# Two seams of a transformer layer: the last values' copy behind the first weight casts, and the feed-forward's first operands half a token tile sooner

## The chip, the cores and the metric

The kernel runs on one core of a Trainium2 chip. The metric is the device time of one execution in microseconds (us). Three executions of the kernel before took 3070.08, 3070.73 and 3071.90; their median, 3070.73 us, is the time before. One further execution was taken with the profiler; it took 3072.42 us, and its trace spans 3070.6 us.

The core's engines work side by side, each through its own instructions in order: TensorE (PE) multiplies matrices into the PSUM banks, VectorE (DVE) and ScalarE (ACT) do elementwise work, GpSimd (POOL) helps, and the SP queue issues most transfers (DMA). ACT issues a few transfers of its own.

## The reference

One layer over 2048 latent tokens of width 1024, with 256 context tokens. Cut to what matters:

```
x = x + g1 * branch_merge(attn_x, gm_x, ga_x, gb_x, w_br_attn, w_br_gm, w_out)

def branch_merge(attn_o, gm_o, ga_logit, gb_logit, w_br_attn, w_br_gm, w_out):
    y = sigmoid(ga_logit) * (attn_o @ w_br_attn) + sigmoid(gb_logit) * (gm_o @ w_br_gm)
    return y @ w_out

h2 = modulate(x, norm2_g, sh2, sc2)          # RMSNorm, scale, shift
x = x + g2 * (square(relu(h2 @ w_ff1)) @ w_ff2)
```

`attn_x` is softmax attention of 8 query heads over 2304 keys; `gm_x` is a gated branch. All data are float32.

## The kernel before

**Precision and products.** Every product of float32 matrices is made of three passes: each operand is split into a high part (a cast, on ACT) and a low part (the difference, on DVE or POOL), and PE adds high x high, high x low and low x high (`mm3`, L181, in the merge; `product`, L1541, in the feed-forward). The feed-forward's matrices are moreover multiplied by a scheme of seven block products: out of the four quarters of each operand come seven sums, numbered 0 to 6, and seven products are taken in the order 0, 1, 5, 6, 4, 2, 3 or near it. Each of these sums is split again into a high and a low half (`halves`, L1359). An operand of the left side has four pieces, one per 128 of the 512 channels (HK = 4).

**Stages.** Projections; attention (`attend`, L1109), in units of one block of 512 tokens and two heads; the merge (`merge`, L1240); then the feed-forward (`ffn`, L1767) in two blocks of 1024 tokens, each as a first half `ff1` and a second half `ff2`.

**The end of the attention.** `values` (L2114) adds the weighted values of a unit in one PSUM bank, `self.o`. `leave` (L2141) copies it to SBUF on ACT and stores it to `at_d` on ACT's queue. For the last unit, this stands at the end of `attend`, directly behind the last values. The merge then begins with loads (`load`), the split of the branch weights of its first step (`cast(0, "dve")`: two casts on ACT, two differences on DVE), and the first weight load for the output product.

**The merge.** For each of four blocks of 512 tokens there are eight steps (branch products, gates, y), and then the output product: four token tiles `tt` of 128 tokens, each in two halves `n` of 512 columns, 24 passes per half. The results are multiplied by a gain and added to the residual row on DVE (L1345, L1346; below called the residual add); when both halves of a row tile are in, `stored` (L1265) writes it to `x1_d` through SP's queue (L1266) and squares it on ACT (L1269). `stored` for tile `tt` is called at `(tt + 1, 0)`, behind that half's products. Between the halves a side generator takes a step, ahead of the residual add of that half (L1341 to L1346).

**The side generator of the last block** is `h_first` (L1403): it prepares the operands of the first feed-forward block from `x1_d`. Piece by piece (`kk`) it loads x (`x1_load`, four transfers, L1377), scales it (`x1_scaled`, one DVE instruction of 128x2048, L1385), transposes it on PE into four banks and copies these to SBUF on ACT with scale and shift (`x1_turned`, L1391, the copy is L1398), and forms the sums (`sums`, L1409). The steps are: load 0; then for each piece "scale, and the sums of the piece before" and "turn, and load the next". `w1_ops` (L1477) prepares the weights of a feed-forward group, also in steps: load (L1482), high and low part of the first half (L1493, L1494), two sums (L1499 to L1504), their splits (L1508, L1509), the last split (L1514, L1515). In `merge` before, the fourth piece is turned, and the weights' first cast made, only behind the merge's last product.

**Order.** Instructions go to each engine's list by a planner that takes them by the order in which the program wrote them, as operands and tile slots come free in its own time model. `order` (L1863) restricts it: instructions of a pinned range keep the written order on every engine, SP's queue included; the merge (to L1352) and ff2 are pinned. In the attention only PE and DVE are held. Instructions behind a pinned range may be pulled forward into it. Tiles of one tag get their slots in written order. `f2` has 16 slots of 2 KB, `wo` 18 of 4 KB (16 for the split output weights, two for their staging), `raw` three. The pool `rest` (operands `hb`, weights `b4`, staging `f9`) lies on the memory that the merge's pool `late` (`y`, `wo`, `xt`, `jk`) gives up.

**ff2 of the first block** has `h_ops` (L1447) beside it, which does for the second block what `h_first` does for the first, five steps per piece. The loads, casts and differences of ff2's own operands are L1648, L1660 and L1661.

Of the kernel before, what the change touches and what calls it, by code (L numbers as in the profile page):

```python
# [30 lines left out]
TB = 512  # L31
NB = SEQ // TB
TT = TB // P
# [12 lines left out]
HK = KC // 2  # L46
# [24 lines left out]
class Kern:  # L71
# [1037 lines left out]
    def attend(self, units, late, mod):  # L1109
        self.psum({"b": 8})  # L1110
        begin = self.here()
        pend = []
        for i, u in enumerate(units):
            at = lambda n: units[n] if 0 <= n < len(units) else None
            nxt, far, old, older = at(i + 1), at(i + 2), at(i - 1), at(i - 2)
            for gi, g in enumerate(range(0, NKT, GROUP)):
                group = range(g, g + GROUP)
                step = nxt if gi < 2 else far
                for j in group:
                    u.first(j)  # L1120
# [12 lines left out]
                if step:  # L1133
                    step.maxima(3)
                for f in pend:
                    f()
                if gi == 0 and far:
                    far.cast()
                if gi == 2 and old:
                    old.sums()  # L1140
                if step:
                    step.maxima(3)
                if gi == 0:
                    if older:
                        older.inverse()
                    if far:
                        far.remainder()
                if gi == 1:
                    if nxt:
                        nxt.reference()  # L1150
                    if old:
                        old.join()
                pend = [lambda u=u, j=j: u.values(j) for j in group]
            pend.append(u.leave)
        for _ in mod:
            pass
# [83 lines left out]
    def merge(self, first, start, last, ops, w1):  # L1240
# [32 lines left out]
        load(0, "gx")  # L1273
        load(1)
        cast(0, "dve")
        next(w_out)
        inp = first
        for b in range(NB):
# [30 lines left out]
            else:  # L1309
# [3 lines left out]
                self.open("back")  # L1313
                side = self.h_first(ops, w1)
            next(side)
            xt, done = x_row(b, 0), None
            for tt in range(TT):
                tok = slice(tt * P, (tt + 1) * P)
# [15 lines left out]
                for n in range(2):  # L1334
                    cs = slice(n * 512, (n + 1) * 512)
                    ps = banks[n]
                    outer(n, range(head if tt == 0 else 0, KC))
                    if n == 0 and done:
                        stored(*done)
                        done = None  # L1340
                    if b + 1 < NB or (tt, n) < (TT - 1, 1):  # L1341
                        next(side, None)
                    next(mod, None)
                    part = self.sb("jk", [512])
                    nc.vector.tensor_tensor(out=part, in0=ps, in1=self.g1b[:, cs], op=ALU.mult)  # L1345
                    nc.vector.tensor_tensor(out=xt[:, cs], in0=xt[:, cs], in1=part, op=ALU.add)  # L1346
# [3 lines left out]
                for _ in side:  # L1350
                    pass
        self.pins.append(range(begin, self.here()))  # L1352
        for _ in range(2):
            next(side)
        self.close("late")
        self.open("rest")
        return side
# [30 lines left out]
    def x1_block(self, blk, r, kk):  # L1388
        return self.x1_scaled(self.x1_load(blk, kk), r)

    def x1_turned(self, x, kk):  # L1391
        nc, raw = self.nc, {}
        for i, j in ((0, 0), (1, 0), (1, 1), (0, 1)):
            ps = self.bank([TB])
            self.transposes(ps, [x[:, i * TT + t, j, :] for t in range(TT)])
            a = raw[i, j] = self.sb("f2", [TB])
            k = kk + j * HK
            nc.scalar.activation(  # L1398
                a, ps, AF.Identity, scale=self.G2[:, k : k + 1], bias=self.S2[:, k : k + 1]
            )  # L1400
        return raw

    def h_first(self, ops, w1):  # L1403
# [3 lines left out]
        keep = {}  # L1407

        def sums(kk, raw):  # L1409
            s1, s2 = (self.sb("f2", [TB]) for _ in range(2))  # L1410
            ops[0][kk] = self.halves(raw[0, 0], 0)
            tt(out=s1, in0=raw[1, 0], in1=raw[1, 1], op=add)
            tt(out=s2, in0=s1, in1=raw[0, 0], op=sub)
            ops[5][kk] = self.halves(s2, 5)
            tt(out=raw[1, 0], in0=raw[0, 0], in1=raw[1, 0], op=sub)
            s4 = s2
            if kk < 2:
                ops[1][kk] = self.halves(raw[0, 1], 1, kk)
                s4 = raw[0, 1]
            keep[kk] = {6: raw[1, 0], 4: s1, 3: raw[1, 1], 2: s4}  # L1420
            if kk >= 2:
                keep[kk][1] = raw[0, 1]
            tt(out=s4, in0=raw[0, 1], in1=s2, op=sub)

        x, raw = self.x1_load(0, 0), None
        yield
        for kk in range(HK):
            self.x1_scaled(x, r)
            if kk:
                sums(kk - 1, raw)  # L1430
            yield
            raw = self.x1_turned(x, kk)
            if kk + 1 < HK:
                x = self.x1_load(0, kk + 1)
            else:
                next(w1)
            yield
        sums(HK - 1, raw)
        next(w1)
        yield  # L1440
        for p in (1, 6, 4, 3, 2):
            for kk in range(HK):
                if p in keep[kk]:
                    ops[p][kk] = self.halves(keep[kk][p], p, kk)
            yield

    def h_ops(self, blk, ops):  # L1447
# [6 lines left out]
        for kk in range(HK):  # L1454
# [9 lines left out]
            tt(out=s2, in0=s1, in1=raw[0, 0], op=sub)  # L1464
# [7 lines left out]
            tt(out=s4, in0=raw[0, 1], in1=s2, op=sub)  # L1472
            ops[3][kk] = self.halves(raw[1, 1])
            ops[2][kk] = self.halves(s4)
            yield

# [512 lines left out]
class Unit:  # L1989
# [148 lines left out]
                    out=self.acc[e][:, h], in0=old[:, h], in1=pt[h], op=ALU.add  # L2138
                )

    def leave(self):  # L2141
        k = self.k
        oc = k.t2([TB])
        self.nc.scalar.copy(oc, self.o)
        self.nc.scalar.dma_start(k.at_d[self.b][self.p * P : (self.p + 1) * P, :], oc)

# [82 lines left out]
```

## Time and profile before

| | |
|---|---|
| median of three executions | 3070.73 us (3070.08 to 3071.90) |
| profiled execution | 3072.42 us, span of its trace 3070.6 us |
| PE busy | 2981.3 us, 97% of the span |
| DVE busy | 2070.4 us, 67% |
| ACT busy | 1457.8 us, 47% |
| POOL busy | 656.7 us, 21% |
| merge, first branch product (L183) | at 1437.49 us |
| merge, last transposes | at 1803.34 us |
| feed-forward, first product | at 1808.64 us |

A row of a timeline shows the start and the length in us, the engine, the line, the operation, the tiles written and read, their shape and how many instructions the row merges; in brackets, how long the engine stood idle before it and what it waited for. PEld is the weight load of PE, SPq and ACTq are the transfers' issues on these queues. Operations on PE overlap, so a product of 0.39 us length follows the one before by less. In the lists of waits the figures are total time, times and longest.

### The profile page before, as it was taken

The page shows a single profiled execution, that of the slowest core. Times are in us where ns is not written, and L with a number is a line of the kernel's source. Part 1 is how long each engine was busy: PE and PEld are TensorE (multiplying, and loading weights), DVE is VectorE, ACT ScalarE, POOL GpSimd, SP SyncE. Part 2 cuts the span into 40 slices and gives each one's busy share as a digit, 9 for nine tenths or more (in the row PEclk, how much of TensorE's full clock was granted, in tenths as well). Part 3 has the DMA queues.
Part 4 walks back from the last instruction along what each step waited for, and adds up shares of the span by engine and source line. Part 5 has one row for each costly group of instructions (what it writes and reads, how often), then busy time and mean ns, then how long its engine had stood idle before and what let it go on. Part 6 is the DMA issues. An engine that isn't in the chain of part 4 may idle for free.

```text
span 3070.6 us, 38002 instructions
## 1 busy us (share of the span) xinstructions
PE 2981.3 (97%) x13501; PEld 2256.5 (73%) x13501; DVE 2070.4 (67%) x3006; ACT 1457.8 (47%) x2350; POOL 656.7 (21%) x488
## 2 busy tenths in 40 slices
PE   6999999989999999999999989999999999999999
PEld 4877788866555555555888878888777888888887
DVE  4876577875887677667655588776576666654555
ACT  5645765653555545545322254444454344444442
POOL 0000000001888888886222200000000000000000
PEclk9999999999999999999999999999999999999999
DMA  8686656644011000004676558888776544448554
GB/s 293 211 268 209 226 191 205 202 152 129 28 36 42 15 5 18 11 8 132 233 214 208 183 171 310 310 302 293 263 227 221 190 152 152 152 152 288 206 206 151
DMA packets 386591, 534.33 MB, mean 174 GB/s; under 512 B 32912, under 2 KB 204096, under 8 KB 386400
## 3 DMA queue, kind: packets, MB, share of 16 engines
q1 hardware_dynamic: 376624, 515.89, 50.4%
q10 hardware_dynamic: 9776, 16.01, 1.4%
q8 instruction: 106, 1.74, 0.2%
q14 instruction: 85, 0.70, 0.1%
HBM read 367.69 MB, written 164.10 MB: 173 GB/s over the span
## 4 chain that ended last, share of the span: by engine, by line
PE 84%; DVE 6%; DMA 5%; ACT 2%; issue 2%; SPq 0%; ACTq 0%; DVEq 0%
PE b L1546 13%; PE b L1545 13%; PE b L1547 13%; PE b L2121 8%; PE b L2088 5%; PE b L2107 4%; PE b L183 4%; PE b L185 4%; PE b L184 4%; PE b L2053 3%; PE a L1545 3%; PE a L1546 3%; PE a L1547 3%; PE b L189 2%; DMA f<-in_w_in 1%
## 5 line engine op out<-in xcount | busy, mean ns | idle before, releaser
L2064 DVE TENSOR_REDUCE ts<-b 128x1 f32<-128x512 f32 x512 | 314.7, 681 | 142.2 <-PE b L2053 142.2
L2137 POOL TENSOR_TENSOR ac<-ac,p 128x512 f32<-128x512 f32 x216 | 300.3, 1423 | 69.4 <-ACT p L2111 68.8
L1661 DVE TENSOR_TENSOR b<-b,b 128x1024 fp32r<-128x1024 f32 x170 | 200.7, 1220 | 128.9 <-ACT b L1660 127.6
L2111 ACT ACTIVATE p<-b 128x512 f32<-128x512 f32 x384 | 199.8, 615 | 167.4 <-PE b L2107 156.2
L1660 ACT CAST b<-b 128x1024 fp32r<-128x1024 f32 x170 | 170.7, 1051 | 225.1 <-PE b L1547 107.9
L1546 PE MATMUL b<-b,b 128*128 128x512 f32 x680 | 266.3, 392 | 5.6 <-DVE b L1661 5.6
L1545 PE MATMUL b<-b,b 128*128 128x512 f32 x680 | 267.1, 393 | 3.3 <-ACT b L1728 1.4
L1547 PE MATMUL b<-b,b 128*128 128x512 f32 x680 | 265.3, 390 | 0.0
L2137 POOL TENSOR_TENSOR ac<-ac,t 128x512 f32<-128x512 f32 x152 | 217.5, 1456 | 0.0
L2088 PE MATMUL b<-h,h 128*128 128x512 f32 x576 | 200.9, 419 | 3.1 <-ACT t L2169 1.7
L2107 PE MATMUL b<-h,h 128*128 128x512 f32 x576 | 180.6, 395 | 0.0
L2121 PE MATMUL b<-p,h 128*64 128x512 f32 x768 | 175.3, 598 | 0.0
L1546 PE MATMUL b<-hb,b 128*128 128x512 f32 x446 | 173.8, 390 | 0.0
L1555 DVE TENSOR_TENSOR f<-f,b 128x512 f32<-128x512 f32 x160 | 109.1, 682 | 82.1 <-issue 48.3
L1545 PE MATMUL b<-hb,b 128*128 128x512 f32 x415 | 161.8, 390 | 0.0
L1547 PE MATMUL b<-hb,b 128*128 128x512 f32 x415 | 161.3, 389 | 0.0
L2010 POOL MEMSET t<- 128x512 f32 x16 | 8.4, 525 | 700.2 <-DMA tb_d<-t 677.9
L1546 PEld LDWEIGHTS b<-b,b 128*128 128x128 f32 x680 | 128.1, 188 | 35.6 <-DVE b L1661 8.9
L1545 PEld LDWEIGHTS b<-b,b 128*128 128x128 f32 x680 | 128.0, 188 | 32.4 <-ACT b L1660 2.5
L2088 PEld LDWEIGHTS b<-h,h 128*128 128x128 f32 x576 | 106.9, 190 | 61.0 <-DVE ts L2064 19.4
L1547 PEld LDWEIGHTS b<-b,b 128*128 128x128 f32 x680 | 128.1, 188 | 26.4
L1558 ACT ACTIVATE f<-f 128x512 f32<-128x512 f32 x96 | 60.5, 630 | 148.8 <-DVE f L1555 148.8
(428 smaller groups left out, 7416.7 us busy)
## 6 DMA issues: line engine op xcount, KB each, us to landing
ao_d<-f SPq DMA_DIRECT2D x224, 256.0 KB
f<-in_w_ff SPq DMA_DIRECT2D x48, 1024.0 KB
b<-ao_d SPq DMA_DIRECT2D x85, 512.0 KB
b<-w2o_d SPq DMA_DIRECT2D x85, 512.0 KB
w2o_d<-f SPq DMA_DIRECT2D x112, 256.0 KB
f<-in_w_in SPq DMA_DIRECT2D x44, 512.0 KB
f<-x_d SPq DMA_DIRECT2D x64, 256.0 KB
hb<-ao_d SPq DMA_DIRECT2D x54, 256.0 KB
```

The lines of the kernel that those rows point to most:

```text
L183: mm(ps, sh, mh, start=start, stop=False)
L1545: mm(ps, wh, hh, start=start and k == 0, stop=False, skip_group_check=True)
L1546: mm(ps, wh, hl, start=False, stop=False, skip_group_check=True)
L1547: mm(ps, wl, hh, start=False, stop=k == len(w) - 1, skip_group_check=True)
L1660: nc.scalar.copy(h, f32(l))
L1661: nc.vector.tensor_tensor(out=l, in0=f32(l), in1=f32(h), op=ALU.subtract)
L2064: nc.vector.tensor_reduce(out=self.mx[:, t, h, c : c + 1], in_=ps[h], axis=AX.X, op=ALU.max)
L2088: self.nc.tensor.matmul(self.pts[j][h], k.KA[c][self.kv][:, ks], self.qa[h], start=True, stop=False, skip_group_check=True,)
L2107: self.nc.tensor.matmul(s, k.KB[c][self.kv][:, ks], self.qb[h], start=False, stop=True, skip_group_check=True,)
L2111: self.nc.scalar.activation(pt[h], s, AF.Exp)
L2121: nc.tensor.matmul(self.o[h * HD : (h + 1) * HD, :], k.V[c][:, i, self.kv * HD : (self.kv + 1) * HD], pt[h], start=j == 0, stop=j == NKT - 1,)
L2137: nc.gpsimd.tensor_tensor(out=self.acc[e][:, h], in0=old[:, h], in1=pt[h], op=ALU.add)
```

## The change

1. In `attend`, the last unit no longer appends `leave`. `merge` calls it, behind `cast(0, "dve")` and before `next(w_out)`, with a tile of tag `raw` in place of one of tag `t2`.
2. In `merge`, the side generator of the last block takes one more step before the products (so load 0 and the scale of piece 0), takes a step at every half, the last included, and none behind the merge. So each step of `h_first` stands one half tile earlier: turns at n=0, "scale and sums" at n=1. The first weights' load comes with the turn of the fourth piece at `(3, 0)`, their first cast and the sums of the fourth piece at `(3, 1)`. These now lie inside the pinned range.
3. `x1_turned` puts two of the four quarters of a piece of the first block into a slot of tag `wo`, and `sums` is rewritten so that each piece keeps four `f2` tiles (before: four or five, beside temporaries). For pieces 2 and 3 the second operand's halves and the operations for operand 2 come in a step of their own behind the merge.
4. In `h_ops`, the three steps with sums are regrouped: each difference is formed one step before its halves.

```diff
@@ attend
-            pend.append(u.leave)
+            if not u.last:
+                pend.append(u.leave)
@@ merge
         cast(0, "dve")
+        last.leave(self.sb("raw", [TB]))
         next(w_out)
...
             next(side)
+            if b + 1 == NB:
+                next(side)
             xt, done = x_row(b, 0), None
...
-                    if b + 1 < NB or (tt, n) < (TT - 1, 1):
-                        next(side, None)
+                    next(side, None)
...
         self.pins.append(range(begin, self.here()))
-        for _ in range(2):
-            next(side)
         self.close("late")
@@ x1_turned
-    def x1_turned(self, x, kk):
+    def x1_turned(self, x, kk, first=False):
         nc, raw = self.nc, {}
+        if first:
+            two = self.sb("wo", [2, TB])
+            raw[0, 0], raw[1, 0] = two[:, 0], two[:, 1]
         for i, j in ((0, 0), (1, 0), (1, 1), (0, 1)):
             ps = self.bank([TB])
             self.transposes(ps, [x[:, i * TT + t, j, :] for t in range(TT)])
-            a = raw[i, j] = self.sb("f2", [TB])
+            if (i, j) not in raw:
+                raw[i, j] = self.sb("f2", [TB])
+            a = raw[i, j]
@@ h_first, sums
-            s1, s2 = (self.sb("f2", [TB]) for _ in range(2))
-            ops[0][kk] = self.halves(raw[0, 0], 0)
-            tt(out=s1, in0=raw[1, 0], in1=raw[1, 1], op=add)
-            tt(out=s2, in0=s1, in1=raw[0, 0], op=sub)
-            ops[5][kk] = self.halves(s2, 5)
-            tt(out=raw[1, 0], in0=raw[0, 0], in1=raw[1, 0], op=sub)
-            s4 = s2
+            a, b, c, d = (raw[ij] for ij in ((0, 0), (0, 1), (1, 0), (1, 1)))
+            s1, s3 = (self.sb("f2", [TB]) for _ in range(2))
+            ops[0][kk] = self.halves(a, 0)
+            tt(out=s1, in0=c, in1=d, op=add)
+            tt(out=s3, in0=a, in1=c, op=sub)
+            tt(out=a, in0=s1, in1=a, op=sub)
+            ops[5][kk] = self.halves(a, 5)
+            keep[kk] = {1: b, 6: s3, 4: s1, 3: d, 2: b}
             if kk < 2:
-                ops[1][kk] = self.halves(raw[0, 1], 1, kk)
-                s4 = raw[0, 1]
-            keep[kk] = {6: raw[1, 0], 4: s1, 3: raw[1, 1], 2: s4}
-            if kk >= 2:
-                keep[kk][1] = raw[0, 1]
-            tt(out=s4, in0=raw[0, 1], in1=s2, op=sub)
+                ops[1][kk] = self.halves(b, 1, kk)
+                tt(out=b, in0=b, in1=a, op=sub)
@@ h_first, after the pieces
+        next(w1)
         sums(HK - 1, raw)
-        next(w1)
-        yield
-        for p in (1, 6, 4, 3, 2):
+        yield
+        for kk in range(2, HK):
+            k = keep[kk]
+            ops[1][kk] = self.halves(k[1], 1, kk)
+            tt(out=k[2], in0=k[1], in1=k[6], op=add)
+            tt(out=k[2], in0=k[2], in1=k[3], op=sub)
+        yield
+        for p in (6, 4, 3, 2):
             for kk in range(HK):
-                if p in keep[kk]:
-                    ops[p][kk] = self.halves(keep[kk][p], p, kk)
+                ops[p][kk] = self.halves(keep[kk][p], p, kk)
             yield
@@ h_ops
-            ops[0][kk] = self.halves(raw[0, 0], 0)
             tt(out=s1, in0=raw[1, 0], in1=raw[1, 1], op=add)
             tt(out=s2, in0=s1, in1=raw[0, 0], op=sub)
+            ops[0][kk] = self.halves(raw[0, 0], 0)
+            tt(out=s3, in0=raw[0, 0], in1=raw[1, 0], op=sub)
+            yield
             ops[5][kk] = self.halves(s2, 5)
-            yield
             ops[1][kk] = self.halves(raw[0, 1], 1, kk)
-            tt(out=s3, in0=raw[0, 0], in1=raw[1, 0], op=sub)
-            ops[6][kk] = self.halves(s3)
-            yield
-            ops[4][kk] = self.halves(s1)
             tt(out=s4, in0=raw[0, 1], in1=s2, op=sub)
             ops[3][kk] = self.halves(raw[1, 1])
+            yield
+            ops[4][kk] = self.halves(s1)
+            ops[6][kk] = self.halves(s3)
             ops[2][kk] = self.halves(s4)
             yield
@@ Unit.leave
-    def leave(self):
+    def leave(self, oc=None):
         k = self.k
-        oc = k.t2([TB])
+        if oc is None:
+            oc = k.t2([TB])
```

More of the change, by code (lines that the diff above doesn't have):

```diff
@@ L1431, in h_first @@
             yield
-            raw = self.x1_turned(x, kk)
+            raw = self.x1_turned(x, kk, True)
             if kk + 1 < HK:
@@ L1461, in h_ops @@
             s1, s2, s3, s4 = (self.sb("f2", [TB]) for _ in range(4))
-            ops[0][kk] = self.halves(raw[0, 0], 0)
             tt(out=s1, in0=raw[1, 0], in1=raw[1, 1], op=add)
             tt(out=s2, in0=s1, in1=raw[0, 0], op=sub)
+            ops[0][kk] = self.halves(raw[0, 0], 0)
+            tt(out=s3, in0=raw[0, 0], in1=raw[1, 0], op=sub)
+            yield
             ops[5][kk] = self.halves(s2, 5)
-            yield
             ops[1][kk] = self.halves(raw[0, 1], 1, kk)
-            tt(out=s3, in0=raw[0, 0], in1=raw[1, 0], op=sub)
-            ops[6][kk] = self.halves(s3)
+            tt(out=s4, in0=raw[0, 1], in1=s2, op=sub)
+            ops[3][kk] = self.halves(raw[1, 1])
             yield
             ops[4][kk] = self.halves(s1)
-            tt(out=s4, in0=raw[0, 1], in1=s2, op=sub)
-            ops[3][kk] = self.halves(raw[1, 1])
+            ops[6][kk] = self.halves(s3)
             ops[2][kk] = self.halves(s4)
```

## The prediction

> **What bounds the kernel now.** I read the page's busy shares and the chain of waits first.
>
> ```profile
> span 3070.6 us, 38002 instructions
> ...
> PE 2981.3 (97%) x13501; PEld 2256.5 (73%) x13501; DVE 2070.4 (67%) x3006; ACT 1457.8 (47%) x2350; POOL 656.7 (21%) x488
> ...
> PE 84%; DVE 6%; DMA 5%; ACT 2%; issue 2%; SPq 0%; ACTq 0%; DVEq 0%
> ```
>
> TensorE is busy for 97% of the span, so only its idle places and its slow-clock places can pay. The change touches three of them, found in the list of waits and then in the timeline: the start of the merge, the start of the feed-forward, and the second block's operands inside the first ff2.
>
> **Part 1, the copy of the last values.** Timeline around the first seam (SP, PE, DVE, ACT), then two stretches by engine (length, PE, PEld, DVE, ACT, POOL, granted clock, DMA share, GB/s):
>
> ```profile
> 1406.99 0.39 SPq L1221 DMA_DIRECT2D bw<-in_w_br_gm  x1
> ...
> 1433.44 2.35 DVE L2154 TENSOR_TENSOR raw<-ac,ac 128x512 f32<-128x512 f32 x2 [2.39 <-POOL ac L2137]
> ...
> 1433.86 1.89 PE L2121 MATMUL b<-h,h 128*64 128x512 f32 x8
> ...
> 1435.81 0.59 ACT L2144 COPY t<-b 128x512 f32<-128x512 f32 x1 [4.56 <-PE b L2121]
> ...
> 1436.82 2.34 ACT L150 CAST bw<-bw 128x512 fp32r<-128x512 f32 x4 [0.42 <-ACT t L2144]
> ...
> 1437.49 0.50 PE L183 MATMUL b<-in,bw 128*128 128x512 f32 x1 [1.75 <-ACT bw L150]
> ...
> 1437.00:1443.00 6.00, 5.51 (x16) 4.11 (x17) 3.19 (x5) 2.11 (x4) 0.00 (x0) 0.72 0.65 225
> ...
> 2131.00:2137.00 6.00, 5.25 (x23) 4.36 (x24) 2.96 (x3) 2.11 (x2) 0.00 (x0) 1.00 0.92 332
> ```
>
> PE ends the last values at 1433.86 + 1.89 = 1435.75 and stands until 1437.49, because ACT's queue holds the values' copy, its store and only then the first weight cast. The raw weights were issued at 1406.99. ACT idles 4.56 us before the copy. With the copy behind the casts, both casts (2 x 0.6) fit into that idle time, and PE's wait of 1.75 goes. What is late next is the low half on DVE, which follows the join of the last sums (1433.44 + 2.35 = 1435.8); it ends 0.7 later, about 1436.5, and the third product is due at 1435.75 + 2 x 0.23 = 1436.2 (0.23 a product: 23 in 5.25 us at 2131): 0.3 left, as much as that product waits today. The stretch after the gap ran at clock 0.72: 5.51 x 0.28 = 1.5 us more, which I take to go with the gap. Sum: -1.75 - 1.5 = **-3.25**. Bounds: if the casts' tiles lie on memory that the last values still read, the cast starts at 1435.75, the gain is 1.75 - 0.7 = 1.05 and the slow stretch stays; so -1.05 to -3.25, and I take the upper end because ACT's row names only its own queue as the wait.
>
> The copy moves behind two casts, its store on ACT's queue with it. Behind them wait the casts of step 1, due 24 products (24 x 0.23 = 5.5 us) after 1435.75; they start near 1436.8 as now: nothing. The `raw` slot in place of a `t2` one costs nothing while the three `raw` tiles hold two sums and this copy; the next is taken at the third step. The `t2` tile no longer lies under the merge's first gate loads, so SP's queue runs somewhat ahead. POOL is not moved past anything.
>
> Sentences that stand alone: the Trainium skill, "TensorE: Matmul & The Clock Gate", Part 1 (the HAM clock gate), says that the clock falls to half after at least one idle window of about 3.4 us. By that rule a gap of 1.75 us would not cause the slow stretch, the 1.5 us would stay, and the total would come out 1.5 us higher, at 3065.2, still inside the forecast's own span. Here the clock was 0.72 after a gap of 1.75 and 1.00 after one of 0.95 at 2131, so the row speaks for a shorter gap being enough.
>
> **Part 2, the first feed-forward operands.** PE at the second seam, and the stretch's clock:
>
> ```profile
> 1803.34 1.91 PE L189 MATMUL b<-ident,f 128*128 128x128 f32 x16
> ...
> 1808.64 0.79 PE L1545 MATMUL b<-in,f 128*128 128x512 f32 x1 [3.38 <-ACT f L1493]
> ...
> 1814.94 0.40 PE L1545 MATMUL b<-in,b 128*128 128x512 f32 x1
> ...
> 1820.30 0.51 PE L1545 MATMUL b<-in,b 128*128 128x512 f32 x1 [3.12 <-ACT in L1367]
> ...
> 1826.72 0.40 PE L1546 MATMUL b<-hb,b 128*128 128x512 f32 x1
> ...
> 1805.00:1825.00 20.00, 11.81 (x33) 8.05 (x32) 16.02 (x23) 13.39 (x23) 0.00 (x0) 0.74 0.48 161
> ```
>
> The transposes of the fourth piece end at 1805.25; the first three operands' products (36) are through at 1826.72. At 0.23 each they need 8.3 us: 13.2 us are lost, by two waits and the clock. The change takes the pieces half a token tile earlier, so the fourth is turned before the last 24 products, and the first weights' cast and the fourth sums stand inside the last half tile.
>
> But look where each half tile's DVE work stands. Today scale and sums come at n=0, and the residual add of n=1, which the row store waits for, follows at once. After the change they come at n=1, ahead of that add; and in SP's written order the store (L1266) stands ahead of the next piece's load (L1377), and of the first weights' load (L1482). Rows of today's cycle, DVE, ACT, SP, and DMA activity in slices of 0.3 us from 1778 and from 1790:
>
> ```profile
> 1767.56 2.28 DVE L1385 TENSOR_TENSOR f<-f,fs 128x2048 f32<-128x2048 f32 x1
> ...
> 1770.45 0.69 DVE L1368 TENSOR_TENSOR in<-f,in 128x512 fp32r<-128x512 f32 x1 [0.61 <-ACT in L1367]
> ...
> 1776.41 0.69 DVE L1346 TENSOR_TENSOR xt<-xt,jk 128x512 f32<-128x512 f32 x1
> ...
> 1766.08 2.79 ACT L1398 ACTIVATE f<-b,S,G 128x512 f32<-128x512 f32 x4 [10.26 <-PE b L189]
> ...
> 1767.66 0.33 SPq L1266 DMA_DIRECT2D x_d<-xt  x1
> ...
> 1779.68 0.33 SPq L1266 DMA_DIRECT2D x_d<-xt  x1
> 1780.11 2.64 SPq L1377 DMA_DIRECT2D f<-x_d  x4
> ...
> 1792.34 0.33 SPq L1266 DMA_DIRECT2D x_d<-xt  x1
> 1792.77 0.38 SPq L1482 DMA_DIRECT2D f<-in_w_ff  x1
> ...
> DMA  0000000079999579999999999421000000000000
> ...
> DMA  0000000000599899699999999930000000000000
> ```
>
> From store to landed piece: 1779.68 to about 1786.1 (slice 27), 6.4. From store to landed weights: 1792.34 to 1798.1, 5.8. A scale is 2.28; from a piece's first low half to the end of the n=1 add, 1776.41 + 0.69 - 1770.45 = 6.65 (5.4 for a piece without the second operand's two ops). New cycle, in today's times: piece 0 is turned three products sooner, ACT ends its four copies near 1768.1, a cast of 0.6, first low half at 1768.7, store at 1768.7 + 6.65 = 1775.3 (today 1767.66). Piece 2 lands 1781.7, scaled 1784.0, store 1790.6 (today 1779.68). Piece 3 lands 1797.0, scaled 1799.3, store 1804.7 (today 1792.34). The weights land at 1804.7 + 5.8 = **1810.5**, 12.4 us later than today. PE turns piece 3 at 1799.3 instead of 1797.9; that 1.4 is hidden behind the weights. With the cast (1.06, next row) the first product comes at 1811.6, 2.9 **later** than today. Its operands are indeed ready sooner; its weights are not.
>
> What follows depends on how the planner fills DVE while the weights are awaited:
>
> ```profile
> 1795.54 0.64 ACT L1367 CAST gx<-f 128x512 fp32r<-128x512 f32 x1
> ...
> 1807.53 1.06 ACT L1493 CAST f<-f 128x1024 fp32r<-128x1024 f32 x1
> ...
> 1807.67 0.69 DVE L1368 TENSOR_TENSOR in<-f,in 128x512 fp32r<-128x512 f32 x1 [2.72 <-ACT in L1367]
> ...
> 1809.42 1.22 DVE L1494 TENSOR_TENSOR f<-f,f 128x1024 fp32r<-128x1024 f32 x1
> ...
> 1822.71 3.81 DVE L1368 TENSOR_TENSOR hb<-f,hb 128x512 fp32r<-128x512 f32 x6
> ```
>
> Filled: the later halves of pieces 0 to 2 go before the weights, and then 6.3 us for the first operand (1808.64 to 1814.94 again) and 24 x 0.23 = 5.5 give 1811.6 + 11.8 = 1823.4 against 1826.72: -3.3. Not filled: before the second operand PE needs the copy of the first product, which needs the third `f2` slot to come free (2 + 2 tiles of each of four pieces fill all 16). DVE's list up to there, after the weights: 4 ops of 128x1024 (4 x 1.22 = 4.9) and 18 of 128x512 (five of the fourth sums, two residual adds, two of the weights, two low halves, four for the seventh operand, three low halves of `6`) at 3.81/6 = 0.64: 11.5. So 1810.5 + 16.4 = 1826.9, 12 products of 0.23 more, 1829.7: +3.0. The row at 1795.54 is a cast of the ff stage that the planner did pull into the merge; the one at 1807.67 is a hole of 2.72 that it left. Between the two I take **-0.7**.
>
> The 16 tiles, in return, end today's shortage (18 wanted); the `wo` staging is free since the first block: nothing. Four p=2 ops instead of two are in the list above.
>
> **Part 3, the second block's operands** (h_ops, beside ff2). PE's waits there, and ACT:
>
> ```profile
> 2230.82 0.62 ACT L1367 CAST in<-f 128x512 fp32r<-128x512 f32 x1 [5.30 <-DVE f L1464]
> ...
> 2234.84 0.50 PE L1546 MATMUL b<-b,b 128*128 128x512 f32 x1 [0.94 <-DVE b L1661]
> ...
> 2275.88 0.50 PE L1546 MATMUL b<-b,b 128*128 128x512 f32 x1 [0.86 <-DVE b L1661]
> ...
> 2323.41 0.50 PE L1545 MATMUL b<-b,b 128*128 128x512 f32 x1 [0.36 <-ACT b L1660]
> 2324.87 0.50 PE L1546 MATMUL b<-b,b 128*128 128x512 f32 x1 [0.95 <-DVE b L1661]
> ```
>
> ACT waits for a difference that DVE has just begun (5.30), and the ff2 casts stand behind that cast. After the change each cast's source is made one step earlier, so ACT does not wait. The ops and steps are the same in number. All four waits could go: 0.94 + 0.86 + 0.36 + 0.95 = **-3.1**. Bounds: 0 (the second step now has three casts instead of two, 0.6 more ahead of the ff2 casts) to -3.1; I take the full value, as a step of 24 products (5.5 us) holds 3 x 0.6 + 2.0 of ACT.
>
> **Sum.** -3.25 - 0.7 - 3.1 = -7.05. The profiled execution took 3072.42, so 3065.4; against the median of 3070.73 it is 3063.7.
>
> **The rivals.**
>
> A, the operands do come sooner: if the weights landed before 1804, PE would go on at 1805.25 and save up to 13.2 there. For it: nothing but DVE's idle time in the merge. Against it: the store cycle, which would have to be 6 us shorter over three rounds. 3.25 + 13.2 + 3.1 = 19.6: 3051; half of it 3057.
>
> B, the hole stays unfilled: +3.0 at the second seam, total -3.35: 3067.4. For it 1807.67, against it 1795.54.
>
> C, slower: the weights for ff2. Their first load starts today at 1806.49, released by the square of the last row:
>
> ```profile
> 1806.49 0.37 SPq L1524 DMA_DIRECT2D f<-in_w_ff  x1
> ...
> SPq L1524 <- ACT jk L1269: 1.1, 1, 1.1
> ```
>
> Its tile lies on the merge's scratch. The last row's add now stands behind the fourth sums: 1811.6 + 1.2 + 5.4 = 1818.2, square 1.1: 1819.3, 12.8 later. If SP's queue then stands on the seven stores of that load with the next weights behind it, PE loses what exceeds its slack; if all 12.8 came through, -3.25 - 3.1 + 12.8 = +6.5: 3077.2. It decides from a delay of 6.4 past the slack on. Against it: no PE wait between 1826 and 2131 today.
>
> **How the numbers follow.** 0.2% (6.1 us) is about what a measurement of this kernel can tell from no change. Forecast (3061 to 3067) 0.50; A 0.12; B 0.20; C and other mishaps of its size 0.18. Faster than 3064.6: A and 0.36 of the forecast, 0.48. Slower than 3076.8: most of C, 0.15. The rest, 0.37, is same. The range leaves out the best of A and the worst of C: 3055 to 3076.
>
> **What would show it.** Seam 1: the first L183 near 1435.8 with no ACT wait and clock near 1. Seam 2: row stores (L1266) 8 to 12 us later against PE, the first L1482 after the third store, PE idle 4 us or more for the L1493 cast. ff2: no L1661 wait at the h_ops steps. Wrong if L1482 is issued before the third store, or if DVE fills the wait wholly.

## The result and the profile after

The changed kernel takes 3076.12 us (median of 20 executions, 3072.20 to 3082.49) beside 3072.03 us of the kernel before (20 executions, 3067.66 to 3081.18). The ratio is 1.0012, with a 95% interval of 1.0003 to 1.0020: slower by about 4 us, where some 7 us less had been forecast, and inside the 0.2% that I had called no change.

The page of the kernel after, its span, busy shares and chain:

```profile
span 3071.2 us, 38003 instructions
...
PE 2976.4 (97%) x13501; PEld 2249.2 (73%) x13501; DVE 2068.9 (67%) x3008; ACT 1457.5 (47%) x2350; POOL 657.8 (21%) x488
...
PE 81%; DMA 7%; DVE 7%; ACT 3%; issue 2%; SPq 1%; POOL 0%; DVEq 0%; ACTq 0%; POOLq 0%
```

The two spans (3070.6 and 3071.2) hide the loss. Up to the last values the two programs are the same on PE, yet that shared part ended at 1435.75 in the profile before and at 1431.01 (1429.12 + 1.89, below) in the profile after. It differs by chance between executions (three kernels below that are the same program up to there, e7, e12 and e14, have 1436.77, 1433.11 and 1435.84), by more than what is looked for. So everything below is counted from the end of the last values (V), and each stage ends at an event of PE's timeline: the first product of operand 1 (the third operand that PE takes), the first wait for a low half of ff2, the same in the second block, and the end. How far these stages repeat can be read from kernels that share a stage's program: five profiles with part 1 and without part 2 (e5, e7, e10, e12, e14 below) have 384.04 to 384.36 from V to operand 1, while ff1 has 308.66 to 309.83 in the four kernels with the same ff1 (before, e5, e6, e7). So a difference in ff1 of about 1 us between two profiles says nothing.

| us | V to operand 1 | ff1, to the first ff2 wait | ff2, to the second block's | to the end | V to end |
|---|---|---|---|---|---|
| before | 387.34 | 308.66 | 632.98 | 305.87 | 1634.85 |
| after | 393.07 | 312.00 | 629.10 | 306.02 | 1640.19 |
| difference | +5.73 | +3.34 | -3.88 | +0.15 | +5.34 |

**First seam.** PE, ACT, and the stretch by engine (length, PE, PEld, DVE, ACT, POOL, granted clock, DMA share, GB/s), after:

```profile
1429.12 1.89 PE L2129 MATMUL b<-h,h 128*64 128x512 f32 x8
1430.93 0.50 PE L183 MATMUL b<-in,bw 128*128 128x512 f32 x1
...
1427.11 1.14 ACT L150 CAST bw<-bw 128x512 fp32r<-128x512 f32 x2 [0.60 <-DMA sm_d<-t]
1431.07 0.59 ACT L2153 COPY raw<-b 128x512 f32<-128x512 f32 x1 [2.83 <-PE b L2129]
...
1430.00:1436.00 6.00, 5.96 (x26) 3.91 (x23) 4.23 (x7) 1.73 (x3) 0.00 (x0) 1.00 0.94 291
```

The casts run in ACT's idle time, the copy waits for the values behind them, the first branch product follows the last values at once, and the clock, 0.72 in the stretch before, is 1.00.

**Second seam.** SP, DVE, PE, two stretches, and what SP's queue waited for between 1760 and 1830, after:

```profile
1768.13 0.33 SPq L1267 DMA_DIRECT2D x_d<-xt  x1
...
1784.79 0.33 SPq L1267 DMA_DIRECT2D x_d<-xt  x1
...
1799.36 0.33 SPq L1267 DMA_DIRECT2D x_d<-xt  x1
1799.79 0.38 SPq L1490 DMA_DIRECT2D f<-in_w_ff  x1
...
1775.91 2.29 DVE L1386 TENSOR_TENSOR f<-f,fs 128x2048 f32<-128x2048 f32 x1 [6.49 <-DMA f<-x_d]
...
1791.80 2.29 DVE L1386 TENSOR_TENSOR f<-f,fs 128x2048 f32<-128x2048 f32 x1 [5.71 <-DMA f<-x_d]
...
1806.81 1.23 DVE L1502 TENSOR_TENSOR f<-f,f 128x1024 fp32r<-128x1024 f32 x1 [6.15 <-ACT f L1501]
...
1778.26 1.97 PE L189 MATMUL b<-ident,f 128*128 128x128 f32 x16 [0.69 <-DVE f L1386]
...
1794.15 1.97 PE L189 MATMUL b<-ident,f 128*128 128x128 f32 x16 [3.01 <-DVE f L1386]
...
1806.83 0.79 PE L1553 MATMUL b<-in,f 128*128 128x512 f32 x1 [5.23 <-ACT f L1501]
...
1818.00 0.79 PE L1553 MATMUL b<-in,b 128*128 128x512 f32 x1 [5.28 <-ACT b L1516]
...
1794.00:1801.00 7.00, 6.85 (x39) 5.95 (x40) 5.87 (x10) 2.25 (x4) 0.00 (x0) 1.00 0.13 46
1799.00:1819.00 20.00, 9.45 (x26) 5.96 (x24) 13.06 (x19) 9.76 (x15) 0.00 (x0) 0.77 0.47 158
...
SPq L1267 <- DVE xt L1349: 49.5, 4, 13.0
```

This is a ring: SP's queue stands at the row store until DVE has made the residual add (up to 13.0 us); the next piece's load, and at last the weights, stand behind the store; and DVE, in its written order, stands on that load (6.49 and 5.71) before it scales, sums and only then makes the next add. PE now waits inside the merge (0.69 and 3.01), then 5.23 for the first weights and 5.28 for the second operand's. In the kernel before, no PE wait lay between the halves.

**ff2.** PE's waits after the first ff2 wait, to 2780 (line, what was waited for, total, times, longest), of before and of after:

```profile
PE b L1546 <- DVE b L1661: 4.7, 5, 1.0
PE b L1545 <- ACT b L1728: 1.4, 1, 1.4
PE b L1545 <- ACT b L1660: 1.0, 2, 0.6
PE b L1545 <- DVE f L1682: 0.9, 1, 0.9
```

```profile
PE b L1554 <- DVE b L1669: 3.4, 3, 1.5
PE b L1553 <- ACT b L1736: 1.3, 1, 1.3
PE b L1553 <- DVE f L1690: 0.9, 1, 0.9
PE b L1553 <- ACT b L1668: 0.6, 1, 0.6
```

### The profile page after: what moved, and what is told of

Read it like the earlier page. It is cut to its first block, busy times and chain, and to the rows that moved or that the text cites. A ratio compares the mean times of both kernels' runs of the same rounds, so it can differ in the third digit from the quotient of the medians.

```text
span 3071.2 us, 38003 instructions
## 1 busy us (share of the span) xinstructions
PE 2976.4 (97%) x13501; PEld 2249.2 (73%) x13501; DVE 2068.9 (67%) x3008; ACT 1457.5 (47%) x2350; POOL 657.8 (21%) x488
## 4 chain that ended last, share of the span: by engine, by line
PE 81%; DMA 7%; DVE 7%; ACT 3%; issue 2%; SPq 1%; POOL 0%; DVEq 0%; ACTq 0%; POOLq 0%
PE b L1553 13%; PE b L1554 13%; PE b L1555 13%; PE b L2129 8%; PE b L2096 5%; PE b L2115 4%; PE b L183 3%; PE b L185 3%; PE b L184 3%; PE b L2061 3%; PE a L1553 3%; PE a L1554 3%; PE a L1555 3%; PE b L189 2%; DMA f<-in_w_in 1%
```

## The experiments

My theory after the result (W): the ring above, that is, the row's add behind the sums on DVE and the store ahead of the loads on SP, makes part 2 a loss. Rivals: the ff2 weights' late load (C of the prediction), and the first weights' load alone.

**The parts apart.** Part 2 alone (e1), part 1 alone (e5), part 3 alone (e6), parts 1 and 3 (e7): the diff of the change above with the other parts left as before. In short:

```diff
 e1: without   last.leave(self.sb("raw", [TB]))   and with h_ops as before
 e5: before  + last.leave(self.sb("raw", [TB]))   behind cast(0, "dve")
 e6: before  + h_ops regrouped
 e7: e5      + h_ops regrouped
```

> Part 2 alone: before, with the side generator of the last merge block one step ahead, the wo staging and the new sums; the last values' copy and h_ops as before. Stage measured: from the end of the last values to the first product of operand 6 (391.0 before: 1435.75 to 1826.72; 396.0 in the changed kernel: 1431.0 to 1826.95), and from there to the first ff2 wait (305.0 before, 309.1 changed). Theory W (the row store, now behind the sums, holds the loads and the first weights in SP's queue): the copy's 3.2 us are missing, so 399 here, and 309 behind it: +8 to +12 us against before. Rival N (the loss is spread over the runs and not in this part): stage near 391, time within 3 us of before.

> Part 1 alone on the kernel before. Stages: from the end of the last values to the first product of operand 1 (387.3 before), from there to the first wait of ff2 (308.7), from there to the same wait of the second block (633.0), the rest 305.9. The theory of the prediction: the gap of 1.75 and the slow-clock stretch go, the first stage is 384.1 (3.25 less), the others do not change; about 3 us below before. Rival, by the clock rule: the slow stretch stays, 385.6.

> Part 3 alone on the kernel before (the regrouped operand steps of the second block). Theory: only the third stage moves, from 633.0 to 629 (the four waits of 3.1 us in sum and a slow-clock stretch), about 4 us below before. Rival: these waits depend on when ff2 begins, that is on the seams, and the stage stays within 1 us of 633.

> The changed kernel with part 2 undone: the copy behind the casts and the regrouped second block, the first operands as before. Theory W: the two gains add, 384.1 and 629 in the first and third stage, 308.7 and 306 in the others: 7 us below before, 11 below the changed kernel. Rival (the parts need each other): less than 4 us below before.

| us | V to operand 1 | ff1 | ff2 | V to end | ratio to before (95%) |
|---|---|---|---|---|---|
| e1, part 2 | 395.66 | 312.92 | 634.70 | 1649.27 | 1.0043 (1.0026 to 1.0059) |
| e5, part 1 | 384.13 | 309.01 | 632.61 | 1631.97 | 0.9989 (0.9980 to 0.9998) |
| e6, part 3 | 387.36 | 309.43 | 628.72 | 1631.62 | 0.9988 (0.9979 to 0.9997) |
| e7, parts 1 and 3 | 384.07 | 309.83 | 628.65 | 1628.63 | 0.9972 (0.9961 to 0.9983) |

Part 1 gains 3.2 in the first stage, part 3 gains 4.3 in ff2, and e7 has both. Part 2 alone costs 8.3 at the seam and 4.3 in ff1; ff2 is 1.7 longer beside it, which stays unexplained. The 14.4 from V to the end are more than the 8 to 12 expected of W.

**The ring cut open.** e2 writes the row store behind the side step in the last block, so the next piece's load no longer stands behind it; e3 leaves the store and puts the add at n = 1 ahead of the scale and sums; e4 leaves both and only asks for the first weights half a tile earlier.

```diff
 e2 (last block)
-                    if n == 0 and done:
-                        stored(*done)
-                        done = None
                     next(side, None)
+                    if n == 0 and done:
+                        stored(*done)
+                        done = None
 e3 (last block, n == 1, tt < 3)
-                    next(side, None)
                     nc.vector.tensor_tensor(out=xt[:, cs], in0=xt[:, cs], in1=part, op=ALU.add)
+                    next(side, None)
 e4
                 sums(kk - 1, raw)
+            if kk + 1 == HK:
+                next(w1)
             yield
...
-            else:
-                next(w1)
             yield
```

> The changed kernel with one edit: in the last merge block the row store of a token tile is written behind the side step of that half, so that the next piece's load and the first weights' load stand ahead of it in SP's queue. DVE's order is not touched. Theory W: DVE's waits of 6.5 and 5.7 for loads go, PE's waits of 0.7 and 3.0 at the turns go, the first weights are issued before the third store and the first product's wait of 5.2 goes; the stage from the last values' end to operand 6 falls from 396 to 383 to 387, the time is 9 to 13 us below the changed kernel. Rival D (DVE's longer list behind the sums is what binds): the waits move to the second operand (5.3 now, up to 10 then), stage 390 to 394, time 2 to 6 us below the changed kernel.

> The changed kernel with one edit: in the last merge block, at the second half of the first three token tiles, the residual add is written ahead of the side step, so that the row store need not wait for scale and sums. SP's order is not touched. Theory W: the stores come back to within 2 us behind their half's last product, loads and weights with them, no load wait of DVE over 2 us, first product without its 5.2: stage 383 to 388, 8 to 13 us below the changed kernel. Rival D: as with the store behind the side step, 390 to 394. Rival S (the scale, which now waits for the half's last product, comes too late for the next turn): PE waits of 1 us or more at the turns remain.

> The changed kernel with one edit: the first weights' load is written half a tile earlier, with the scale of the fourth piece, ahead of the third row store in SP's queue; the pieces' own loads stay behind the stores. Theory W with both parts of the loss: PE's waits at the turns (3.7) stay, the weights' cast follows the copies of the fourth piece, first product about 2.5 us sooner, second operand too: stage 392 to 394, 2 to 4 us below the changed kernel. Rival F (the late first weights are the whole loss): both waits of 5.2 and 5.3 go, stage 386.

| us | V to operand 1 | ff1 | V to end | ratio to before (95%) |
|---|---|---|---|---|
| after | 393.07 | 312.00 | 1640.19 | 1.0012 (1.0003 to 1.0020) |
| e2, store behind | 381.78 | 312.12 | 1629.42 | 0.9981 (0.9971 to 0.9990) |
| e3, add first | 383.70 | 313.02 | 1631.97 | 0.9980 (0.9971 to 0.9990) |
| e4, weights early | 390.76 | 314.11 | 1640.15 | 1.0010 (1.0000 to 1.0019) |

SP and PE at the seam of e2:

```profile
1783.99 0.33 SPq L1267 DMA_DIRECT2D x_d<-xt  x1
1784.94 0.37 SPq L1493 DMA_DIRECT2D f<-in_w_ff  x1
...
1812.28 0.80 PE L1556 MATMUL b<-in,b 128*128 128x512 f32 x1 [6.52 <-ACT b L1519]
```

The weights are asked for at 1784.94, 20.4 us sooner against V than in after (348.36 to 368.78), PE does not wait in the merge, and the first product comes with no wait. Cutting the ring on either engine brings 9.4 to 11.3 us at operand 1 and 8.2 to 10.8 to the end, so W is shown. The weights' load alone, with PE's turn still waiting 3.48, brings 2.3 at operand 1 and nothing to the end (1640.15 beside 1640.19), where 2 to 4 had been expected. What is left in e2 is the wait of 6.52 for the second operand's weights, whose sums stand behind the fourth piece's sums and the add on DVE.

**The fourth sums first.** e8 is e2 with the first weights' cast and low half in the middle of the fourth sums instead of ahead of them, so that DVE fills its hole.

```diff
+            next(between, None) if between else None
             ops[5][kk] = self.halves(a, 5)
...
-        next(w1)
-        sums(HK - 1, raw)
+        sums(HK - 1, raw, w1)
```

> The changed kernel with the row store behind the side step, and the fourth piece's sums written ahead of the first weights' cast, which comes between them (operand 0's halves, three differences, the weights' cast and low part, operand 5's halves). Claim: with the weights there in time DVE's list behind the fourth piece binds, and DVE's wait of 3.8 for the weights' cast is the part of it that can be filled. Then the second operand's wait of 6.5 falls to 3 to 5, the first stage from 381.8 to 379 to 380, the time is 2 to 3 us below the kernel with only the store moved. Rival (the weights' sums behind the residual add bind, whatever stands before): wait 6 to 7 still, no change of time.

V to operand 1 380.69, ff1 313.03, V to end 1629.40; ratio 0.9968 (0.9957 to 0.9980). Of the 2 to 3 us expected beside e2, 1.1 came at operand 1 and none to the end (e2: 1629.42). PE's row in e8:

```profile
1808.82 0.51 PE L1556 MATMUL b<-in,b 128*128 128x512 f32 x1 [4.04 <-ACT b L1519]
```

The wait falls from 6.52 to 4.04 and operand 1 comes 3.4 us sooner than in e7, which has no part 2. Yet to the first ff2 wait e8 needs 380.69 + 313.03 = 693.7 and e7 384.07 + 309.83 = 693.9. All versions with part 2 and all its work have this longer ff1 (312.0 to 314.1 in after, e1 to e4 and e8), so even mended it gains nothing.

**Why ff1 gives it back.** First I held DVE's list of ff1's first groups for the cause. e9 (on e8) and e10 (on e7) move the low halves of operands 3 and 2 to POOL, which is idle there:

```diff
-                ops[p][kk] = self.halves(keep[kk][p], p, kk)
+                lo = self.nc.gpsimd if p in (3, 2) else None
+                ops[p][kk] = self.halves(keep[kk][p], p, kk, lo)
```

> The kernel with the store moved and the fourth sums first, and one more edit: the eight low halves of operands 3 and 2 of the first block are formed on POOL, which is idle there, and not on DVE. Claim B (what part 2 gains at the seam is given back in ff1's first groups, because DVE's list there is the bound): with eight instructions of 0.6 less on DVE the stage from operand 1's first product to ff2 falls from 313.0 to 309 to 310.5, the first stage (380.7) stays or falls by up to 1; the time is 2 to 4 us below the kernel without this edit. Rival P (the longer ff1 stage comes from the second weights' later load, or from the transfers): the stage stays at 312 to 313. Rival Q (POOL's operations, some 1.4 us each, come too late for operand 3, or slow DVE): it grows.

> The same eight low halves on POOL in the kernel with parts 1 and 3 alone. Claim B: PE does not wait for DVE behind operand 1 there (0.6 in all), so DVE's time is free: the stage stays at 309 to 310, the first at 384, and the time within 1.5 us of the kernel with parts 1 and 3.

ff1 316.56 and 317.80; ratios 0.9986 (0.9977 to 0.9994) and 1.0006 (0.9997 to 1.0015): worse in both, where DVE's operations on SBUF are slower beside POOL (last section), so they settle nothing on DVE's list. e11 (on e8) and e12 (on e7) therefore leave out work of DVE instead, the 24 differences in the first six groups of output weights. The stores stay, of plain quarters, and wait for no difference, and four `f2` tiles of each group are not taken; these two kernels, and e13 and e14 below, do not compute the layer.

```diff
+        if s < 6:
+            yield
+            yield
+            for p, src in enumerate((b11, b21, b22, b21, b12, b22, b22)):
+                nc.sync.dma_start(self.wo_d[p][s // 2][s % 2], src)
+            yield
+            return
```

> The fourth sums' kernel, with the four differences of w2_ops left out for its first six groups: it stores the loaded quarters in the places of the seven operands, so the output weights' operands are wrong there. That takes 24 VectorE operations of 0.68 us (16.4 us) out of the first groups of the feed-forward and leaves every transfer, product and ScalarE operation. If VectorE's backlog makes the first feed-forward stage 3 to 4 us longer once the first operands come sooner, the stage from operand 1's first product to the first wait of the second product falls from 313.0 to 309 to 310.5 us, and TensorE's waits on L1566 (1.6 us) go. If the weights of the next tiles or the transfers hold it, the stage stays at 312 to 313 us.

> The same left out of the kernel with parts 1 and 3 alone (the output weights' operands of the first six groups are again quarters as loaded). There the stage has 309.8 us and TensorE's waits after the first operands are 0.6 us: if VectorE's backlog matters only beside the earlier operands, this stage stays within 0.8 us of 309.8; if the backlog binds the first feed-forward groups in every version, it falls by as much as in the run before, by 3 us or so.

ff1 311.42 and 308.42: 1.6 and 1.4 us less, each 0.6 or less below the lowest of its kind. So DVE's list does not make the difference, which stays at 3.0; whether it costs both something can't be told. (Ratios 0.9973, 0.9963 to 0.9982, and 0.9980, 0.9970 to 0.9989.) The casts of ff1's weights showed another lead. ACT in e7, then in e8, the seventh and eighth group:

```profile
1907.03 1.05 ACT L1495 CAST b<-f 128x1024 fp32r<-128x1024 f32 x1 [2.77 <-DMA f<-in_w_ff]
1924.61 1.05 ACT L1495 CAST b<-f 128x1024 fp32r<-128x1024 f32 x1 [2.95 <-DMA f<-in_w_ff]
```

```profile
1904.79 1.05 ACT L1504 CAST b<-f 128x1024 fp32r<-128x1024 f32 x1 [5.74 <-DMA f<-in_w_ff]
1922.21 1.05 ACT L1504 CAST b<-f 128x1024 fp32r<-128x1024 f32 x1 [4.33 <-DMA f<-in_w_ff]
```

Counted from V they stand at 470.3 and 487.8 in e7 and at 470.6 and 488.0 in e8: the weights land at the same time, though operand 1 begins 3.4 us sooner in e8. e13 (on e8) and e14 (on e7) take transfers away and no instruction of PE, DVE or ACT:

```diff
         for p, src in enumerate((b11, b21, b22, t4, t1, t2, t3)):
+            if s < 6 and p > 2:
+                continue
             nc.sync.dma_start(self.wo_d[p][s // 2][s % 2], src)
...
-        for src in (self.ao_d[blk][p][c], self.wo_d[p][c]):
+        for src in (self.ao_d[blk][p][c], self.wo_d[0 if c < 3 and p > 2 else p][c]):
```

> The fourth sums' kernel, with four of the seven stores that w2_ops makes left out for its first six groups (the three quarters as loaded are still stored, all four differences are still computed on VectorE, and the later load takes the stored first operand in place of the four that are missing, so the output weights' operands are wrong there). That is 24 stores of 256 KB less in the first six groups, and not one instruction less on TensorE, VectorE or ScalarE. If transfers keep the pace of the first feed-forward groups, the seventh to ninth casts of weights no longer wait 4 to 6 us for their load and the stage from operand 1's first product to the first wait of the second product falls from 313.0 to 309 to 311 us. If it is VectorE's list, the stage stays at 312.5 to 313.5 us.

> The same 24 stores left out of the kernel with parts 1 and 3 alone, where the stage has 309.8 us and the casts wait 2.8 to 3.4 us: if transfers are what gives the earlier operands' gain back, this stage falls by at most 1.5 us, and the kernel of the run before becomes 1.5 to 3 us the faster of the two, counted from the end of the last values to the first wait of the second product (both have 693.7 to 693.9 us with all stores). If not, the two stay within 1 us of each other in that sum.

The loads of these two groups, the same two casts and the stretch from 1900 to 1930 (columns as above) in e13, then the loads and that stretch in e8:

```profile
1896.02 0.45 SPq L1493 DMA_DIRECT2D f<-in_w_ff  x1
...
1914.54 0.45 SPq L1493 DMA_DIRECT2D f<-in_w_ff  x1
...
1901.55 1.05 ACT L1504 CAST b<-f 128x1024 fp32r<-128x1024 f32 x1 [0.58 <-DMA f<-in_w_ff]
...
1920.28 1.05 ACT L1504 CAST b<-f 128x1024 fp32r<-128x1024 f32 x1 [0.16 <-DMA f<-in_w_ff]
...
1900.00:1930.00 30.00, 30.00 (x133) 24.75 (x132) 23.89 (x32) 14.90 (x22) 0.00 (x0) 1.00 0.70 248
```

```profile
1896.03 1.08 SPq L1493 DMA_DIRECT2D f<-in_w_ff  x1
...
1915.40 0.65 SPq L1493 DMA_DIRECT2D f<-in_w_ff  x1
...
1900.00:1930.00 30.00, 28.69 (x125) 23.03 (x124) 21.61 (x28) 13.46 (x19) 0.00 (x0) 1.00 0.86 310
```

The transfers' share falls from 0.86 to 0.70, and PE's three waits of 2.5 us in all that stand behind the late casts in e8 (479 to 512 from V, put down to ACT and DVE) are gone. ff1 is 309.86 in e13, 3.2 less and clear of the spread; 308.49 in e14 is not. From V to the first ff2 wait it is 380.34 + 309.86 = 690.2 and 384.36 + 308.49 = 692.9. With fewer stores e8's kernel is 2.7 us ahead of e7's; with all of them it is level. So what the stores do to the weights' loads takes back most of what the earlier operands bring. This rests on one profile of each: the ratios, 0.9963 (0.9948 to 0.9978) and 0.9969 (0.9958 to 0.9980), do not tell e13 from e14.

How the stores do it, the traces show in part. Counted from V, the load that the seventh cast waits for is issued at 461.8 in e8 and 458.3 in e13, and lands 8.7 and 5.5 us later; for the eighth it is 481.2 and 476.8, then 6.8 and 5.7. So the loads are asked for sooner on SP's queue, where the stores stand ahead of them, and they also land faster; which counts more was not taken apart. A store that is left out also frees its `f2` tile sooner. e11, which never takes these tiles and keeps every store, gained only 1.6, so this is hardly the whole.

Of the complete kernels e7 (0.9972) and e8 (0.9968) are the best, and both are faster than before and than the change; they can't be told from each other. I would keep e7, the simpler one.

## Why the prediction was right or wrong, point by point

**Part 1, -3.25: right.** V to operand 1 falls by 3.2 in e5. The gap of 1.75 is gone, the third product's weight load waited 0.47 for DVE's low half (0.43 in the kernel before) where 0.3 was forecast, and the slow stretch went with the gap, as taken from the row: had it stayed, the gain would have been 1.5 less.

**Part 2, -0.7: wrong, and this step carries the whole miss.** Against e7 the change loses 393.07 - 384.07 = 9.0 at the seam and 2.2 in ff1. The chain of events was the forecast one (stores late, weights behind the third store, PE idle for the weights' cast, DVE's hole unfilled); its sizes were not:
- "From store to landed piece, 6.4": 7.8 (1768.13 to 1775.91) and 7.0 (1784.79 to 1791.80). Around the ring, the third store comes 368.35 - 353.31 = 15.0 us later against V than in e7, not 12.4.
- "That 1.4 is hidden behind the weights": PE's turns waited 0.69 + 3.01 = 3.7 inside the merge, and that is not hidden. The weights' load is written behind the fourth turn and the third store, so a late turn pushes the weights too. The merge's last product stands 6.1 us later than in e7: 3.7 of waits, 1.9 for the 16 transposes that moved in, 0.5 left over. Then come 5.23 of waiting for the weights, as long as the transposes and the wait in e7 (1.9 + 3.39). So the first product is 6.2 later, not 2.9.
- From there to operand 1 it takes 17.25 instead of 14.46: waits of 5.28 and 0.34 against 0.83, 3.12 and 0.85 in e7, the rest at a granted clock of 0.62 against 0.74 over that stretch. I had both ends of this step ("filled", "not filled") with today's clock.
- The value -0.7 lay between a filled (-3.3) and an unfilled hole (+3.0), a little to the filled side. DVE's hole of 6.15 decides for the unfilled one: the casts and low halves that could fill it are written behind the weights inside the pinned range. The row at 1795.54 that I had set against it is of work behind that range, and the row of 2.72 was the nearer one. And +3.0, taken as the end of the range, lacked the turn's wait and the clock.

**Part 3, -3.1: right in kind, too small.** ff2 is 3.9 shorter in after and 4.3 in e6. The waits at 2275.88 and 2323 to 2325 are gone; the one of 0.94 at 2234.84 stayed and has 1.48 in after, while e6 and e7, with the same steps, do not have it, so the bound that I had named (one more cast ahead) is not shown to be its cause. The lists of waits lose 1.8 in after and 3.4 in e6. The rest in after, 2.1, is as much as the clock would give (2% of 100 us): 0.98 before and 1.00 after from 2134 to 2234; in e6 the clock is 0.98 as before, and 0.9 stay unexplained.

**The sum** of -7.05 became +5.3 by the stages: 9.0 instead of -0.7 at the seam, and ff1's +3.3, which no term had: the sum put at nothing what earlier operands do to a stage whose weights' loads stand among stores (up to 1.2 of it is the spread of this stage).

**The rivals.** B's hole stayed unfilled, with three times its price. A is refuted as it was argued, by the store cycle; even where experiments lifted that cycle, its gain of 13.2 did not come: the second operand's weights held PE next (6.52 in e2), and ff1 was longer. (Its half gain gives 3057.8, not 3057.) C's delay came as worked out (the load at 1814.48, 12.7 us later against V), but not its price: e2 has that load only 1.4 later and the same ff1.

## What to carry to other kernels

When a step moves inside a hand-written order, follow the ring it may close: a store that waits for an engine, loads behind that store on the same queue, and that engine waiting for the loads. The delay of one turn comes back each time around, and here it was ended by writing the store behind the loads, or the add ahead of the sums. Before an operand is brought sooner, ask whether the stage that it feeds waits for loads that stand among stores; then an earlier start may buy only an earlier wait, as here, where e8 and e7 are level within 0.2 us at the end of ff1. And where the time between executions moves by as much as the effect, count stages from an event that both programs share.

## What was not expected of the hardware

**POOL slows DVE's operations on SBUF.** DVE and POOL of e9, and two such DVE rows of e8:

```profile
1819.35 4.91 POOL L1372 TENSOR_TENSOR hb<-f,hb 128x512 fp32r<-128x512 f32 x3 [74.27 <-ACT hb L1371]
1824.70 9.12 POOL L1372 TENSOR_TENSOR hb<-f,hb 128x512 fp32r<-128x512 f32 x5 [0.45 <-ACT hb L1371]
...
1824.73 1.82 DVE L1547 TENSOR_TENSOR f<-f,f 128x512 f32<-128x512 f32 x1
1826.48 2.31 DVE L1506 TENSOR_TENSOR b<-f,b 128x1024 fp32r<-128x1024 f32 x1
...
1830.94 0.67 DVE L1567 TENSOR_TENSOR f<-f,b 128x512 f32<-128x512 f32 x1
```

```profile
1822.37 1.22 DVE L1505 TENSOR_TENSOR b<-f,b 128x1024 fp32r<-128x1024 f32 x1 [1.27 <-ACT b L1504]
...
1827.66 0.68 DVE L1546 TENSOR_TENSOR f<-f,f 128x512 f32<-128x512 f32 x1
```

While POOL works, a difference of two SBUF tiles takes 1.82 instead of 0.68 and 2.31 instead of 1.22; the one at 1830.94, which reads a PSUM bank, keeps 0.67. By the timeline eight DVE operations were slowed, by some 6.8 us together, against 5.1 us (8 x 0.64) for the eight low halves that POOL took over. The Trainium skill, "SBUF — State Buffer", section "SBUF: two separate sides", says that a DVE operation with two SBUF inputs and a GpSimd operation that reads SBUF exclude each other for a whole instruction; the rows agree, the PSUM one too.

**The clock.** In the kernel before, the clock was still 1.00 in the 1.6 us behind PE's gap of 1.75; it fell to 0.55 at 1439, had 0.59 until 1443 and 1.00 again from there, which makes the 0.72. In the kernel after, it stayed at 1.00 behind the gap of 3.01 (1794 to 1801), though the gaps of 5.23 and 5.28 brought a mean of 0.77. The same transposes stand behind slightly longer gaps in e1 and in e4:

```profile
1799.87 3.56 PE L189 MATMUL b<-ident,f 128*128 128x128 f32 x16 [3.19 <-DVE f L1384]
```

```profile
1800.63 3.68 PE L189 MATMUL b<-ident,f 128*128 128x128 f32 x16 [3.48 <-DVE f L1386]
```

They take 1.97 us behind the gap of 3.01, 3.56 behind 3.19 and 3.68 behind 3.48 (the clock is 0.50 at their start in both). Among these three the length of the gap could decide; with the gap of 1.75 it does not. The Trainium skill, "TensorE: Matmul & The Clock Gate", Part 1, speaks of an idle window of about 3.4 us; the gaps of 3.01 and 3.48 agree, that of 3.19 is near it, that of 1.75 does not agree, and what else counted there stays open.
